# Log-sum-exp of 16,384 rows: 116 rows to a partition and 12 read last, instead of 112 and 16

## The chip, the cores and the metric

The kernel runs on one NeuronCore of one Trainium2 chip. The metric is the device time of one execution in microseconds (us). Before the change the median of three runs is 162.66 us (162.47 to 162.76). A profile adds one more execution, recorded by the hardware profiler.

Engines are named as in the profile: ACT (ScalarE: the exponentials and logarithms), DVE (VectorE: the sums), PE (TensorE: here only a tiny check), SP (SyncE, which issues the transfers; its queue is written SPq). Transfers run on 16 DMA engines of the core.

## The reference

The input has 32 x 512 = 16,384 rows of 1,024 float32 numbers (67.1 MB); the output is one float32 for each row.

```python
def reference(x):
    max_x = np.max(x, axis=-1, keepdims=True)
    return max_x.squeeze(-1) + np.log(np.sum(np.exp(x - max_x), axis=-1))
```

## The kernel before

**What it computes.** It takes exp without subtracting the maximum, sums each row and takes the logarithm. A check at the end looks whether every sum lies between 1e-15 and 1e15. If one doesn't, a slow path recomputes everything with the maximum; with the input used here it isn't taken.

**Rows and partitions.** There are 128 rows for each of 128 partitions (`NC = 128`; a row is 4 KB). `B` splits them. With B = 16, partition p holds rows 112p to 112p + 111 of the first 14,336 rows of the input (`x_rows`), so that its data begins 448 KB after that of partition p - 1. The last 2,048 rows of the input (`x_rest`) are spread 16 to a partition, and here partitions are 64 KB apart. `W = NC - B = 112` is the border, counted in rows of one partition; a load must lie on one side of it (the assertion in `source`). The output is cut in the same way, `out_rows` and `out_rest`.

**Loads.** The list `LOADS` gives eighteen transfers, all issued from SP into one ring of 48 rows for each partition. Each fetches the same number of rows for all 128 partitions, as one piece of consecutive bytes for each partition. I number them 1 to 18. Loads 1 to 4 have 16 rows (a 64 KB piece for a partition), load 5 has 13.5, load 6 12.5, load 7 9, load 8 7.5, load 9 5.5; that is 112 rows. Behind the border come 4.625 (load 10), 3.3125 (11), 2.4375 (12), 1.8125 (13), 1.3125, 0.9375, 0.5625, and the last row in two pieces of 0.625 and 0.375 (17 and 18). SP waits, before it issues a load, until the ring rows that it overwrites have been read (`load`).

**Work.** The string beside each size says what is done with the rows. "R8" is one exp on ACT over 8 rows and one reduction on DVE (lines 192 and 196). "T4" is one exp on ACT and four instructions on DVE, one for each row, each of which adds the halves of a row and accumulates (line 204). "A" is a single row where ACT accumulates the sum itself (line 181). "Y" and "Z" are the two pieces of the last row (line 170). The last exp of a load runs to the end of what has landed, so it may go over part of the row that the next load completes. ACT waits for a load's semaphore before its first exp.

**The end.** When row 119 of a partition (`LATE`) is summed, an early logarithm over the first W rows is put into ACT's order (line 219; it waits for the sums of the rows below the border), and the check of the first 119 sums into DVE's. SP then stores `out_rows` (line 227). After the last rows there are the logarithm of the other rows but one (line 230), that of the last row (line 232), the store of `out_rest` (line 236), and, beside these, the check of the last sums over DVE and PE. The program ends when the store has landed and the check has been read.

Of the kernel before, what the change touches and what calls it, by code (L numbers as in the profile page):

```python
# [8 lines left out]

LOW, HIGH = 1e-15, 1e15  # L10
RING = 48
B = 16
LATE = 119


# [1 line left out]
LOADS = [  # L17
# [4 lines left out]
]  # L22

# [24 lines left out]
def kernel(  # L48
# [21 lines left out]
    H = d // 2  # L70
    W = NC - B
    LAST = NC - 1
# [290 lines left out]
```

## Time and profile before

| what | us |
|---|---|
| median of three runs | 162.66 |
| profiled execution | 163.04 |
| its span, from the first to the last instruction | 161.7 |
| DVE busy | 117.7 |
| ACT busy | 116.9 |
| share of the span in which the 16 DMA engines moved the kernel's data | 97.2% |

The profiled execution took 1.3 us more than its span, and 0.38 us more than the median of the runs. Times in the views are counted from the start of the span. In the timeline a row is: start, duration, engine, line, operation, output and input with their shapes, count, and in brackets how long the engine was idle before and what it waited for. Where ACT was idle for a load, the start of its exp tells when that load landed, to some 0.02 us.

### The profile page before, as it was taken

To read this page: it belongs to the slowest core of one execution; us is meant where nothing else is said; L and a number is where in the kernel's file an instruction comes from. 1 tells how busy PE (TensorE), PEld (TensorE's weight loads), DVE (VectorE), ACT (ScalarE), POOL (GpSimd) and SP (SyncE) were. 2 spreads that over 40 slices of the span, in tenths; PEclk is the share of its full clock that TensorE was granted. 3 is DMA by queue.
4 is the path that set the end of the run, shared out by engine and by line. 5 is a ranking of instruction groups with operands and counts; after the bars stand their busy time and mean duration, and the time that the engine had idled before them with its cause. 6 is when DMAs were issued, how large, how long until landed. Compare 5 with 4: busy or idle time off the path is not lost.

```text
span 161.7 us, 249 instructions
## 1 busy us (share of the span) xinstructions
PE 2.1 (1%) x24; PEld 1.0 (1%) x24; DVE 117.7 (73%) x69; ACT 116.9 (72%) x55; POOL 0.2 (0%) x4
## 2 busy tenths in 40 slices
PE   0000000000000000000000000000000000000022
PEld 0000000000000000000000000000000000000011
DVE  0000000899929999399999999999399956999894
ACT  3000059980899609994299949973999999989986
POOL 0000000000000000000000000000000000000000
DMA  7997997998999899799699999998999999999990
GB/s 276 503 519 324 454 519 324 454 519 373 405 519 422 357 519 454 324 519 454 284 438 438 438 422 405 443 494 368 438 438 441 410 417 418 450 408 418 410 392 15
DMA packets 2881, 67.18 MB, mean 416 GB/s; under 512 B 576, under 2 KB 704, under 8 KB 1344
## 3 DMA queue, kind: packets, MB, share of 16 engines
q1 hardware_dynamic: 2880, 67.18, 97.2%
q14 instruction: 1, 0.01, 0.0%
HBM read 67.11 MB, written 0.07 MB: 415 GB/s over the span
## 4 chain that ended last, share of the span: by engine, by line
DMA 58%; ACT 19%; DVE 16%; another core or an unknown queue 3%; SPq 1%; issue 0%; PE 0%; DVEq 0%
DMA ring<-in_x_dram 58%; ACT ring L192 19%; DVE sumexp L196 15%; DVE ring L204 1%; SPq L126 0%; PE count L147 0%; PE count L248 0%; DVE clamped L242 0%; DVE fine L251 0%; SPq L44 0%; DVEq L44 0%
## 5 line engine op out<-in xcount | busy, mean ns | idle before, releaser
L192 ACT ACTIVATE ring<-ring 128x8192 f32<-128x8192 f32 (+18 forms) x27 | 103.6, 3891 | 41.8 <-DMA ring<-in_x_dram 41.8
L196 DVE TENSOR_REDUCE sumexp<-ring 128x8 f32<-128x8192 f32 (+6 forms) x17 | 102.9, 6107 | 39.2 <-ACT ring L192 39.2
L204 DVE SCALAR_TENSOR_TENSOR ring<-ring 128x512 f32<-128x512 f32 x22 | 14.1, 687 | 1.3 <-ACT ring L192 1.3
L181 ACT ACTIVATE ring<-ring 128x1024 f32<-128x1024 f32 x10 | 10.4, 1042 | 0.0
L114 ACT ACT_TABLE_LOAD x1 | 1.3, 1283 | 1.5 <-PEq L57 1.5
L143 PE MATMUL count<-far,bad 128*1 128x1 f32 x2 | 0.2, 164 | 153.8 <-DVE clamped L138 153.8
L181 ACT ACTIVATION_READ_ACCUMULATOR ring<-ring 128x1 f32 x10 | 1.9, 187 | 0.0
L204 DVE DVE_READ_ACCUMULATOR ring<-ring 128x1 f32 x22 | 1.8, 82 | 0.0
L147 PE MATMUL count<-sumexp,ones 128*1 128x1 f32 x20 | 1.8, 164 | 4.1 <-DVE ring L204 4.1
L170 ACT ACTIVATE last_exp<-ring 128x640 f32<-128x640 f32 (+1 forms) x2 | 1.2, 590 | 0.0
L115 DVE MEMSET ones<- 128x1 f32 x1 | 0.1, 59 | 1.5 <-PEq L57 1.5
L143 PEld LDWEIGHTS count<-far,bad 128*1 128x1 f32 x2 | 0.1, 80 | 153.8 <-DVE clamped L138 153.8
L147 PEld LDWEIGHTS count<-sumexp,ones 128*1 128x1 f32 x20 | 0.8, 81 | 5.1 <-DVE ring L204 4.9
L251 DVE TENSOR_SCALAR fine<-count 1x1 int32<-1x1 f32 x1 | 0.1, 145 | 0.5 <-PE count L147 0.5
L170 ACT ACTIVATION_READ_ACCUMULATOR last_exp<-ring 128x1 f32 x2 | 0.4, 186 | 0.0
L138 DVE SCALAR_TENSOR_TENSOR clamped<-clamped,sumexp 128x119 f32<-128x119 f32 x1 | 0.3, 282 | 0.0
L232 ACT ACTIVATE res<-sumexp 128x1 f32<-128x1 f32 x1 | 0.3, 294 | 0.0
L219 ACT ACTIVATE res<-sumexp 128x112 f32<-128x112 f32 x1 | 0.3, 279 | 0.0
L242 DVE SCALAR_TENSOR_TENSOR clamped<-sumexp 128x9 f32<-128x9 f32 x1 | 0.2, 169 | 0.1
L133 DVE TENSOR_SCALAR clamped<-sumexp 128x119 f32<-128x119 f32 x1 | 0.2, 223 | 0.0
L230 ACT ACTIVATE res<-sumexp 128x15 f32<-128x15 f32 x1 | 0.2, 198 | 0.0
L248 PE MATMUL count<-far,bad 128*1 128x1 f32 x2 | 0.2, 164 | 0.0
(8 smaller groups left out, 0.7 us busy)
## 6 DMA issues: line engine op xcount, KB each, us to landing
ring<-in_x_dram SPq DMA_DIRECT2D x1, 6912.0 KB, 31.8
ring<-in_x_dram SPq DMA_DIRECT2D x1, 6400.0 KB, 26.6
ring<-in_x_dram SPq DMA_DIRECT2D x1, 4608.0 KB, 25.2
ring<-in_x_dram SPq DMA_DIRECT2D x1, 3840.0 KB, 23.6
ring<-in_x_dram SPq DMA_DIRECT2D x1, 2816.0 KB, 26.0
ring<-in_x_dram SPq DMA_DIRECT2D x1, 2368.0 KB, 30.4
ring<-in_x_dram SPq DMA_DIRECT2D x1, 1696.0 KB, 23.1
ring<-in_x_dram SPq DMA_DIRECT2D x1, 1248.0 KB, 25.7
```

What stands on the lines that cost most here:

```text
L114: nc.scalar.preload_act_table_set("natural_log_exp_and_others")
L133: dve.did(nc.vector.tensor_scalar(out=clamped[:, 0:LATE], in0=sumexp[:, 0:LATE], scalar1=LOW, scalar2=HIGH, op0=ALU.max, op1=ALU.min,))
L138: dve.did(nc.vector.scalar_tensor_tensor(out=clamped[:, 0:LATE], in0=clamped[:, 0:LATE], scalar=0.0, in1=sumexp[:, 0:LATE], op0=ALU.bypass ...
L143: pe.did(nc.tensor.matmul(count, lhsT=bad[:, 0:1], rhs=far, start=True, stop=False))
L147: return pe.did(nc.tensor.matmul(count, lhsT=ones, rhs=sumexp[:, c : c + 1], **kw))
L170: at = act.did(nc.scalar.activation(out=last_exp[:, here - p : end - p], in_=ring[:, here:end], func=AF.Exp, accum_out=sumexp[:, LAST : NC ...
L181: at = act.did(nc.scalar.activation(out=v, in_=v, func=AF.Exp, accum_out=sumexp[:, c : c + 1]))
L192: at = act.did(nc.scalar.activation(out=v, in_=v, func=AF.Exp))
L196: who = (dve, dve.did(nc.vector.reduce_sum(out=sumexp[:, c : c + s], in_=rows, axis=AX.X)))
L204: who = (dve, dve.did(nc.vector.scalar_tensor_tensor(out=lo, in0=lo, scalar=1.0, in1=rows[:, r, H:d], op0=ALU.mult, op1=ALU.add, accum_out ...
L219: ln_early = act.did(nc.scalar.activation(out=res[:, 0:W], in_=sumexp[:, 0:W], func=AF.Ln))
L232: ln_last = act.did(nc.scalar.activation(out=res[:, LAST:NC], in_=sumexp[:, NC : NC + 1], func=AF.Ln, bias=sumexp[:, LAST:NC]))
```

## The change

B becomes 12, so that W becomes 116. Partitions of the first part are now 464 KB apart in the input, and those of the rest 48 KB. Load 10 has to end at the border and shrinks to 4 rows; load 11 becomes 3.5625 and load 12 2.8125. The rows up to the end of load 9 (112) and up to the end of load 12 (122.375) are as before, and so are all other sizes and the work on each row. Which rows of the input a load fetches does change, for all loads.

```diff
-B = 16
+B = 12
 LATE = 119
...
-    (4.625, "T4"), (3.3125, "T3"), (2.4375, "T3"), (1.8125, "T2"), (1.3125, "T1"), (0.9375, "T1"),
+    (4, "T4"), (3.5625, "T3"), (2.8125, "T3"), (1.8125, "T2"), (1.3125, "T1"), (0.9375, "T1"),
     (0.5625, "T1"), (0.625, "Y"), (0.375, "Z"),
```

By that the early logarithm covers 116 columns instead of 112, the late one 11 instead of 15. The first store writes 464 bytes for each partition instead of 448, the last store 48 instead of 64. In the instruction streams of the engines nothing else moves: PE and DVE have the same instructions in the same order, ACT and SP the same order with those sizes (and in the slow path, which isn't run, one transfer is cut at another row).

## The prediction

> **What bounds the kernel now.** I read the page's sums first, then ACT's timeline at the moments where it waits for data, then the transfers and the timeline of the last 20 us.
>
> ```profile
> span 161.7 us, 249 instructions
> PE 2.1 (1%) x24; PEld 1.0 (1%) x24; DVE 117.7 (73%) x69; ACT 116.9 (72%) x55; POOL 0.2 (0%) x4
> q1 hardware_dynamic: 2880, 67.18, 97.2%
> DMA 58%; ACT 19%; DVE 16%; another core or an unknown queue 3%; SPq 1%; issue 0%; PE 0%; DVEq 0%
> ```
>
> No engine is busy for three quarters of the span, while the DMA engines are at 97.2%. The chain that ended last names DMA for only 58%, because it walks back through the ring's free rows (DVE's reduction lets SP issue); that doesn't make DVE a bound, since a load is issued well before its data can start to flow. ACT's timeline shows the pace:
>
> ```profile
> 21.83 7.03 ACT L192 ACTIVATE ring<-ring 128x8192 f32<-128x8192 f32 x1 [19.09 <-DMA ring<-in_x_dram]
> 41.17 7.03 ACT L192 ACTIVATE ring<-ring 128x8192 f32<-128x8192 f32 x1 [5.21 <-DMA ring<-in_x_dram]
> 60.52 7.03 ACT L192 ACTIVATE ring<-ring 128x8192 f32<-128x8192 f32 x1 [5.31 <-DMA ring<-in_x_dram]
> 79.88 5.32 ACT L192 ACTIVATE ring<-ring 128x6144 f32<-128x6144 f32 x1 [5.41 <-DMA ring<-in_x_dram]
> 96.30 4.47 ACT L192 ACTIVATE ring<-ring 128x5120 f32<-128x5120 f32 x1 [2.38 <-DMA ring<-in_x_dram]
> 111.60 5.75 ACT L192 ACTIVATE ring<-ring 128x6656 f32<-128x6656 f32 x1 [3.39 <-DMA ring<-in_x_dram]
> 143.97 4.15 ACT L192 ACTIVATE ring<-ring 128x4736 f32<-128x4736 f32 x1 [0.43 <-DMA ring<-in_x_dram]
> ```
>
> Each start is a landing. Loads 2, 3 and 4 (16 rows) took 19.34, 19.35 and 19.36 us: 1.209 us for a row of each partition, or 8.389 MB / 19.35 us = 434 GB/s. Three equal steps speak of a ceiling without disturbance. Load 5 (13.5 rows) took 16.42 us, where 1.209 a row makes 16.32: 0.10 too many. Load 6 (12.5 rows) took 15.30 against 15.11: 0.19 too many. Loads 7 to 10 together (26.625 rows) took 32.37 against 32.19. So the stream runs from the first to the last microsecond, within about 1% of its best pace, and a change of its pace goes into the time one to one.
>
> The end of the span, in the same view:
>
> ```profile
> 148.18 3.03 ACT L192 ACTIVATE ring<-ring 128x3392 f32<-128x3392 f32 x1
> 151.12 0.28 ACT L219 ACTIVATE res<-sumexp 128x112 f32<-128x112 f32 x1
> 151.31 2.27 ACT L192 ACTIVATE ring<-ring 128x2496 f32<-128x2496 f32 x1
> 154.10 1.75 ACT L192 ACTIVATE ring<-ring 128x1856 f32<-128x1856 f32 x1 [0.53 <-DMA ring<-in_x_dram]
> 158.54 0.71 ACT L170 ACTIVATE last_exp<-ring 128x640 f32<-128x640 f32 x1
> 159.91 0.29 ACT L232 ACTIVATE res<-sumexp 128x1 f32<-128x1 f32 x1
> 160.23 0.34 SPq L236 DMA_DIRECT2D out_dram<-res  x1
> ```
>
> From 154.10 on ACT has no gap: load 13's landing, then 6.1 us of ACT work, then the last store. Load 13 is late by its own measure. By the transfers' view load 12 was issued at 125.47 and took 25.7 us (151.17), load 13 at 125.94 and 28.1 us (154.04 to 154.08). That is 2.9 us for 1.8125 rows, which at 1.209 make 2.19. The transfers between 152.1 and 152.5 us name the cause that I suspect, a foreign packet on one DMA engine:
>
> ```profile
> q1 hardware_dynamic: 29, 0.18, 115.0%
> q14 instruction: 1, 0.01, 4.8%
> ```
>
> 4.8% of 16 engines' 0.4 us is 0.31 us of one engine, for fetched instructions.
>
> **The change, part by part.**
>
> *Rows 0 to 111 with partitions 464 KB apart instead of 448 (loads 1 to 9).* The bytes, pieces and order are the same; only addresses move. No row of this trace has the new pitch, so I bound it by loads that step in similar ways. A DMA engine goes from the end of one partition's piece to the start of the next. In loads 1 to 4 that step is 448 - 64 = 384 KB, six times 64 KB exactly. In load 5 it is 394 KB, in load 6 398 KB, no multiples of 64 KB, and these are the two long loads that lost time: 0.29 us in 26 rows, 0.011 us a row. With the new pitch loads 1 to 4 step by 400 KB, so they lose that regularity. At 0.011 us a row, 64 rows cost +0.7 us. The rows don't all agree: load 7 steps by 412 KB, was issued at 97.25 and took 25.2 us (to 122.45), which is 10.85 us for 9 rows, no loss at all. The high end is load 6's 0.015 a row over 112 rows, +1.7. Further out lies load 11, 4.22 us for 3.3125 rows (issued 125.09, 23.1 us later landed), 0.065 a row; over 64 rows that would be +4.2. The low end is that all of what loads 5 to 10 lose goes: 0.10 + 0.19 + 0.18 = -0.47. I take +0.7, by loads 5 and 6, the nearest in piece size and the only ones long enough to be measured well.
>
> The Trainium skill's page "DMA: Bandwidth & Descriptors", section "Latency and other measured facts", speaks against this: there, copies slowed down when the row pitch was a large power of two (207 GB/s at 512 KiB, 103 at 4 MiB), and 4 KiB of padding on the 4 MiB pitch brought the full rate back. Neither 448 nor 464 KB is such a power, and 464 KB is divisible by 16 KB at most where 448 is by 64, so by that rule the new pitch is no worse, and the sum would be that of the rivals below, 0 or a gain. The three 19.35 us steps agree that 448 KB does no harm, and no run here shows 464.
>
> *Rows behind the border, partitions 48 KB apart instead of 64, and loads 10 to 12 of other sizes.* The bytes up to load 9 and up to load 12 are the same, so on the old pace load 10 lands 0.625 x 1.209 = 0.76 us earlier (143.2), load 11 0.375 x 1.209 = 0.45 earlier (147.7), and load 12 at 151.17 as before. ACT: load 10's exp is 128x4096 (3.60 us by the row of that shape) from 143.56, where ACT becomes free, to 147.15; then it waits for load 11. That exp is 128x3648: 3.03 + 256 x (4.15 - 3.03)/1344 = 3.24 us, from 147.7 to 150.95. The early logarithm, 116 columns for 112, at the old 0.28. It needs the four sums of load 10; DVE finishes the sums of load 9 at 147.9, then four at 0.61 each, 150.3: no wait. Load 12's exp is 128x2880: 2.27 + 384 x 0.00083 = 2.59 us from 151.19, and leaves ACT free for the next at about 153.70 (successive exps overlap by some 0.08), where before it was free at 153.50. Load 13 lands at 154.08, so this 0.20 is hidden by the wait of 0.53. If that cover goes, because load 13 lands on pace at 151.17 + 2.19 = 153.36, the 0.20 stands in the time in full. I take 0, and keep 0 to +0.2. DVE's three sums behind load 12 then begin at 153.8 instead of 153.67 and end at 155.7; the next ones wait for ACT until 155.89 already. SP's waits for ring rows move with the pieces: loads 11 to 13, issued at 125.09 to 125.94 behind DVE's reduction, begin to flow some 18 us later, and load 10 was issued 30.4 us before it landed. That cover is too large to vanish.
>
> The foreign packet stays, I suppose; instruction streams are nearly the same. If it falls on a DMA engine that is ahead of the others, load 13 lands earlier, and ACT, free at 153.70, gains at most 154.10 - 153.72 = 0.38. I take 0 and keep -0.4.
>
> *The end.* The late logarithm has 11 columns instead of 15, 0.20 us either way (a one-column one took 0.29, by another form). The last store has 48-byte pieces at addresses 48 bytes apart. The old one took 1.4 us from issue to landing; its packets, 144 with 4.6% of 16 engines' 2 us, about 10 ns each. Were each twice as long, nine on an engine would add 0.1; faster by more than a few hundredths it can't be, with less than 0.1 us of packets on an engine. I take 0, and keep 0 to +0.1. The first store, issued behind all loads, landed 7.8 us later at 159.2, before the last one is even issued: nothing.
>
> Sum: +0.7 + 0 + 0 + 0 = +0.7 us on the profiled 163.04, so 163.74. Since the profiled run lies 0.38 above the median, that is 163.36 for the median; I say 163.35.
>
> **The rivals.**
>
> *Pace unchanged.* The stream is at the same ceiling for 64 KB, 36 KB and 30 KB pieces, at five different offsets within a partition, and load 7's odd step costs nothing. Then only the tail is left: 0 to +0.3 us, 162.66 to 162.96. For it: the three equal steps; against it: load 6's 0.19.
>
> *Faster.* The old pitch, 448 KB, puts all partitions at multiples of 64 KB; if the losses of loads 5 to 10 come from engines that meet in the same place of DRAM, addresses spread over multiples of 16 KB take them away. It decides from a loss of under 0.14 us left of the 0.47, and gives up to 162.19 (162.66 - 0.47). This is also where the Trainium skill's rule on row pitch leads when it is taken further than its figures go. Against it: loads 2 to 4 have nothing to gain, and they are half of the stream. The foreign packet on another engine would give the same size, 162.3.
>
> *Much slower.* The new pitch disturbs all loads as load 11 was disturbed: 0.065 x 64 = +4.2, 166.9. Only one short load speaks for it.
>
> **How the numbers follow.** No change means within 0.2%, 0.33 us, about what a measurement of this kernel can tell. Stalls in the first loads, +0.35 to +1.7: 0.42, the forecast. Pace unchanged: 0.28. Faster by 0.33 or more: 0.22, gain of pitch and of packet together. Much slower: 0.08. So faster 0.22, same 0.28, slower 0.50. The range goes from 162.25, which leaves out the far part of the gain, to 164.5 (1.7 for the pitch and the tail's 0.1 or 0.2, on 162.66), which leaves out the much slower case and little else. The forecast case's own range is 163.0 to 164.4.
>
> **What would show it.** In the changed profile ACT's waits for loads 2, 3, 4 should be about 19.5 us apart instead of 19.35; equal steps of 19.35 mean that the pitch costs nothing and that the forecast is wrong. The step from 79.88 to 111.60 (31.72 us for loads 5 and 6) shows the opposite: 31.4 would be the gain. Load 12's exp should start at its landing with load 11's done 0.1 to 0.2 us earlier, and the wait before load 13's exp should shrink from 0.53 to about 0.4. The last store should take 1.4 us to land. What would make me wrong most is the address map of DRAM, of which this trace shows one pitch only.

## The result and the profile after

| | us, median (lowest to highest) |
|---|---|
| before | 162.70 (162.47 to 163.08) |
| after | 163.02 (162.71 to 163.30) |

The ratio is 1.0020, with a 95% interval of 1.0014 to 1.0026: slower by 0.33 us (0.23 to 0.42). The forecast was +0.7, the range 162.25 to 164.5. The sign and the range hold. The mechanism that I had forecast doesn't, as the profile of the changed kernel shows at once. Its execution took 162.97 us. First the page:

```profile
span 161.6 us, 249 instructions
PE 2.1 (1%) x24; PEld 1.0 (1%) x24; DVE 117.5 (73%) x69; ACT 116.7 (72%) x55; POOL 0.2 (0%) x4
q1 hardware_dynamic: 2880, 67.18, 97.2%
DMA 57%; DVE 19%; ACT 18%; another core or an unknown queue 3%; issue 0%; SPq 0%; PE 0%; DVEq 0%
```

The sums agree within 0.2 us, and the DMA engines' share is the same. Then ACT's timeline, where each start is the landing of a load (loads 1 to 6):

```profile
22.30 7.03 ACT L192 ACTIVATE ring<-ring 128x8192 f32<-128x8192 f32 x1 [19.56 <-DMA ring<-in_x_dram]
41.62 7.03 ACT L192 ACTIVATE ring<-ring 128x8192 f32<-128x8192 f32 x1 [5.18 <-DMA ring<-in_x_dram]
60.98 7.03 ACT L192 ACTIVATE ring<-ring 128x8192 f32<-128x8192 f32 x1 [5.32 <-DMA ring<-in_x_dram]
80.33 5.32 ACT L192 ACTIVATE ring<-ring 128x6144 f32<-128x6144 f32 x1 [5.40 <-DMA ring<-in_x_dram]
96.67 4.47 ACT L192 ACTIVATE ring<-ring 128x5120 f32<-128x5120 f32 x1 [2.30 <-DMA ring<-in_x_dram]
111.80 5.75 ACT L192 ACTIVATE ring<-ring 128x6656 f32<-128x6656 f32 x1 [3.22 <-DMA ring<-in_x_dram]
```

Loads 2, 3 and 4 step by 19.32, 19.36 and 19.35 us, where I had written that equal steps of 19.35 mean that the forecast is wrong. The large term, stalls in the first loads, isn't there. Instead load 1 lands 0.47 us later than before (22.30 against 21.83), and loads 5 and 6 together take 31.47 us against 31.72.

The end of ACT's timeline:

```profile
147.79 3.24 ACT L192 ACTIVATE ring<-ring 128x3648 f32<-128x3648 f32 x1 [0.56 <-DMA ring<-in_x_dram]
150.94 0.28 ACT L219 ACTIVATE res<-sumexp 128x116 f32<-128x116 f32 x1
151.25 4.24 ACT L192 ACTIVATE ring<-ring 128x2880 f32<-128x2880 f32 x2
159.43 0.29 ACT L232 ACTIVATE res<-sumexp 128x1 f32<-128x1 f32 x1
```

The last store in SP's timeline:

```profile
159.75 0.34 SPq L236 DMA_DIRECT2D out_dram<-res  x1
```

And the same store in the view of transfers, where the last two columns are its size and the us from issue to landing:

```profile
out_dram<-res SPq DMA_DIRECT2D x1, 6.0 KB, 1.9
```

The last logarithm starts at 159.43, which is 0.48 us *earlier* than in the first profile of before (159.91), and the span is nevertheless hardly shorter (161.6 against 161.7). The last store took 1.9 us where the old one took 1.4. The old one's row, from the first profile of before:

```profile
out_dram<-res SPq DMA_DIRECT2D x1, 8.0 KB, 1.4
```

So two theories stood at this point. **Store:** the 48-byte store lands later, and that is the whole loss. **Pitch:** the 0.4 to 0.5 us at load 1 go through to the end, and the 1.9 is chance. The first profile of before, with its late load 13, was under suspicion in either.

### The profile page after: what moved, and what is told of

It is laid out like the page before. It is cut to its first block, busy times and chain, and to the rows that moved or that the text cites. A ratio compares the mean times of both kernels' runs of the same rounds, so it can differ in the third digit from the quotient of the medians.

```text
span 161.6 us, 249 instructions
## 1 busy us (share of the span) xinstructions
PE 2.1 (1%) x24; PEld 1.0 (1%) x24; DVE 117.5 (73%) x69; ACT 116.7 (72%) x55; POOL 0.2 (0%) x4
## 4 chain that ended last, share of the span: by engine, by line
DMA 57%; DVE 19%; ACT 18%; another core or an unknown queue 3%; issue 0%; SPq 0%; PE 0%; DVEq 0%
DMA ring<-in_x_dram 57%; ACT ring L192 18%; DVE sumexp L196 15%; DVE ring L204 3%; SPq L126 0%; PE count L248 0%; DVE clamped L242 0%; PE count L147 0%; DVE fine L251 0%; SPq L44 0%; DVEq L44 0%
## 5 line engine op out<-in xcount | busy, mean ns | idle before, releaser
L192 ACT ACTIVATE ring<-ring 128x8192 f32<-128x8192 f32 (+17 forms) x27 | 103.3, 3889 | 41.6 <-DMA ring<-in_x_dram 41.5
## 6 DMA issues: line engine op xcount, KB each, us to landing
ring<-in_x_dram SPq DMA_DIRECT2D x1, 1440.0 KB, 25.6
```

The lines of the kernel that those rows point to most:

```text
L192: at = act.did(nc.scalar.activation(out=v, in_=v, func=AF.Exp))
```

## The experiments

Ratios are to the kernel before, run beside each on the same chip.

**r1: the kernel before once more.** No edit.

> The kernel before, unchanged, for a second profile of it. In the first one load 13 landed 2.9 us after load 12 (2.19 on pace) with a foreign packet beside it, load 1 landed at 21.83, and the last store took 1.4 us from issue to landing. Every theory: ratio 1.000 within 0.001. If the late load 13 of the first profile is a matter of where the foreign packet falls, it may be gone here, the span then 161.2 to 161.4; if it belongs to the program, load 13 again lands 2.8 to 2.9 us after load 12. The store theory needs 1.4 us again for the last store.

Ratio 0.9998 (0.9989 to 1.0007), span 161.4. Landings of loads 4 and 6, and the wait ahead of load 13's exp:

```profile
79.87 5.32 ACT L192 ACTIVATE ring<-ring 128x6144 f32<-128x6144 f32 x1 [5.41 <-DMA ring<-in_x_dram]
111.35 5.75 ACT L192 ACTIVATE ring<-ring 128x6656 f32<-128x6656 f32 x1 [3.23 <-DMA ring<-in_x_dram]
153.82 1.75 ACT L192 ACTIVATE ring<-ring 128x1856 f32<-128x1856 f32 x1 [0.64 <-DMA ring<-in_x_dram]
```

Loads 5 and 6 take 31.48 us. All other profiles with the 448 KB pitch have 31.46 to 31.48 too. The 0.29 us that I had read as the price of a step that is no multiple of 64 KB were an event of that one execution, and the "gain" of the changed kernel in these loads was its absence. Load 13 is late again (3.0 us after load 12: 125.22 + 25.6 and 125.69 + 28.1 in the transfers' rows). It isn't in every run: in r3, r6 and r10 below, whose loads are those of before, load 13 comes 2.26 to 2.29 us after load 12, and load 14 is the late one (2.14 to 2.25 us after load 13, where r1 has 1.66). In these three the foreign packet starts at 152.6 to 152.9 us, in the other profiles with this pitch at 150.8 to 152.3. So a late load near the end belongs to the program, and which one it is goes with when the packet comes. The last store took 1.4 us again.

**r2 and r3: the two halves of the change apart.** A second constant cuts the output independently of the input. r2 has the loads of after and the stores of before, r3 the reverse.

```diff
-B = 16
+B = 12          # r2; in r3 B stays 16
+BO = 16         # r2; in r3 12
...
+    WO = NC - BO
-    out_rows = out_flat[0 : P * W].rearrange("(p c) -> p c", p=P)
-    out_rest = out_flat[P * W : n].rearrange("(p c) -> p c", p=P)
+    out_rows = out_flat[0 : P * WO].rearrange("(p c) -> p c", p=P)
+    out_rest = out_flat[P * WO : n].rearrange("(p c) -> p c", p=P)
```

The logarithms and stores use `WO` in place of `W`, and r2 has the sizes of loads 10 to 12 of after.

> Loads of the changed kernel (464 KB and 48 KB pitch, new sizes), stores of the kernel before (448 and 64 bytes for a partition). The sums are right, but are stored at the places of the other cut. Store theory (the 48-byte store costs the 0.45 us that the last store took longer): last store 1.4 us, time as before or slightly less, ratio 0.998 to 1.000. Pitch theory (load 1 lands 0.45 us later because partitions 464 KB apart start worse, and that goes through): ratio 1.002, load 1 at 22.3 us, the store as in the changed kernel or not is of no matter.

> Loads of the kernel before, stores of the changed one (464 and 48 bytes for a partition; early logarithm over 116 columns). The output is permuted. Store theory: last store 1.8 to 1.9 us from issue to landing, ratio 1.002 to 1.003. Pitch theory: last store of 48 bytes is a chance event, ratio 1.000, load 1 at 21.8 us.

r2: 0.9995 (0.9985 to 1.0004). Load 1 landed at 22.2 us, so the late start is there, and the time is that of before. r3: 1.0019 (1.0010 to 1.0028), with load 1 at 21.9. The stores alone cost what the whole change costs, and the loads alone nothing measurable. The transfers' row of the last store in r2, and then in r3:

```profile
out_dram<-res SPq DMA_DIRECT2D x1, 8.0 KB, 1.4
```

```profile
out_dram<-res SPq DMA_DIRECT2D x1, 6.0 KB, 1.6
```

They were issued at 159.73 and 159.77 us; the spans are 161.2 and 161.4. The store theory holds, though r3's 1.6 us is less than the 1.8 to 1.9 that it had asked for, and the pitch theory falls. r3 also has the changed kernel's first store. That one isn't in the way: in the changed kernel's two profiles and in r3 it had landed by 158.74 to 158.83 us, 1.0 us before the last store was issued.

**r4: the sizes of loads 10 to 12 alone.**

```diff
-    (4.625, "T4"), (3.3125, "T3"), (2.4375, "T3"),
+    (4, "T4"), (3.5625, "T3"), (2.8125, "T3"),
```

> The kernel before with loads 10 to 12 of 4, 3.5625 and 2.8125 rows; pitch and stores as before (the load that ends at 116 rows lies behind the border of 112 as the old one did). Store theory and pitch theory: ratio 1.000. Tail theory (ACT is free for load 13 0.20 us later, and the cover of that is absent in most runs): ratio 1.001 to 1.0015, and ACT without a wait ahead of load 13's exp.

Ratio 0.9998 (0.9989 to 1.0007). The wait ahead of load 13's exp shrinks from r1's 0.64 to 0.28 and so still covers the longer exp of load 12:

```profile
153.70 1.75 ACT L192 ACTIVATE ring<-ring 128x1856 f32<-128x1856 f32 x1 [0.28 <-DMA ring<-in_x_dram]
```

The tail theory gives no measurable cost; the 0 that I took for this term stands.

**r5, r6: what makes the store slow.** In r5 the pieces are 48 bytes, but 64 apart; in r6 64 bytes, but shifted by 16.

```diff
# r5
-    nc.sync.dma_start(out=out_rest, in_=res[:, W:NC])
+    nc.sync.dma_start(out=out_rest[:, 4:16], in_=res[:, W + 4 : NC])
# r6
-    out_rest = out_flat[P * W : n].rearrange("(p c) -> p c", p=P)
+    out_rest = out_flat[P * W - 4 : n - 4].rearrange("(p c) -> p c", p=P)
```

> The kernel before, but its last store writes only the last 12 of its 16 columns: pieces of 48 bytes that begin 64 bytes apart, 16 bytes behind a multiple of 64; 512 results are left out. Theory of shared lines (a 48-byte pitch makes pieces of different partitions fall into the same 64 bytes, and their writes get in each other's way): 1.4 us from issue to landing, ratio 1.000. Theory of partial lines (a piece that doesn't fill its 64 bytes is slow by itself): 1.6 to 1.9 us, ratio 1.002.

> The kernel before, but its last store goes to addresses 16 bytes lower, so that each 64-byte piece covers parts of two 64-byte lines and shares both with its neighbours; the first store leaves out 4 columns to make room (432 of 448 bytes for a partition), and some results stand in the wrong place or are missing. Both theories of the store (shared lines, partial lines): 1.6 us or more from issue to landing, ratio 1.001 to 1.003. If only the size of a piece counts: 1.4 us, ratio 1.000.

r5: 1.0000 (0.9991 to 1.0009). r6: 1.0004 (0.9995 to 1.0013). The transfers' row of the store in r5, and then in r6:

```profile
out_dram<-res SPq DMA_DIRECT2D x1, 6.0 KB, 1.4
```

```profile
out_dram<-res SPq DMA_DIRECT2D x1, 8.0 KB, 1.5
```

A piece of 48 bytes isn't slow by itself; the theory of partial lines falls with r5. Pieces that share lines at 64 bytes' length took 0.1 us more in r6, less than both theories had asked for, in one profile and with a time that can't be told from that of before.

**r9, r10: how wide the sharing has to be.** r9 puts the 48-byte pieces 96 bytes apart, r10 shifts the 64-byte pieces by 128 bytes.

```diff
# r9
-    out_rest = out_flat[P * W : n].rearrange("(p c) -> p c", p=P)
+    out_rest = out_flat[P * (W - 8) : n].rearrange("(p c) -> p c", p=P)
...
+    nc.sync.dma_start(out=out_rest[:, 0:12], in_=res[:, W + 4 : NC])
# r10
+    out_rest = out_flat[P * W - 32 : n - 32].rearrange("(p c) -> p c", p=P)
```

> The kernel before, but its last store writes 12 columns as 48-byte pieces that begin 96 bytes apart; the first store writes 104 columns, to make room, and results stand in other places or are missing. Here no two pieces touch the same 64 bytes, but the four neighbouring partitions that one DMA engine should be writing cover 384 bytes, so that blocks of 256 bytes are written by two engines. Theory of shared 64-byte lines: 1.4 us from issue to landing. Theory of blocks of 256 bytes (or 512) that two DMA engines write at once: 1.5 to 1.9 us.

> The kernel before, but its last store goes to addresses 128 bytes lower: 64-byte pieces that fill whole 64-byte lines as before, while the 256 bytes of four neighbouring partitions now straddle two blocks of 256. The first store leaves out 32 columns; results stand in other places. Theory of shared 64-byte lines: 1.4 us from issue to landing, as before. Theory of blocks of 256 bytes that two DMA engines write at once: 1.5 to 1.9 us.

r9: 1.0003 (0.9993 to 1.0013), r10: 1.0001 (0.9991 to 1.0010). Both stores took 1.4 us, so blocks of 256 bytes written from two sides don't matter. Taken together, with places counted from the start of the output:

| last store | run | two pieces in the same 64 bytes | issue to landing, us |
|---|---|---|---|
| 64 bytes, 64 apart | before, r1, r2, r4, r7, r11, r12 | no | 1.4 in each |
| 48 bytes, 48 apart | after, r3, r8 | yes | 1.9, 1.6, 1.6 |
| 48 bytes, 64 apart | r5 | no | 1.4 |
| 48 bytes, 96 apart | r9 | no | 1.4 |
| 64 bytes, 64 apart, shifted 128 | r10 | no | 1.4 |
| 64 bytes, 64 apart, shifted 16 | r6 | yes | 1.5 |

In the trace each store's semaphore is raised sixteen times, once for each DMA engine. The first raise comes 1.25 to 1.27 us after the issue in all of them. The last comes 1.40 to 1.43 us after it without shared lines, 1.52 us in r6, 1.61 us in r3 and r8 and 1.86 us after the change. So some of the engines get their confirmation late (later than 1.43 us: 8 of the sixteen after the change, 7 in r3 and in r8, 2 in r6), and the rest aren't touched. Sharing a 64-byte line is a condition that fits every row of the table. Lines of 32 bytes would fit as well, since the pieces that share 64 bytes here share 32 too, and no run separates the two; lines of 128 bytes wouldn't, since the 64-byte pieces of before share those and took 1.4 us. The place that the store reads from isn't the cause: r5 and r9 read the same 48 bytes of each partition as the changed kernel. Why it costs 0.1 us at 64 bytes and 0.2 to 0.45 at 48 stays open.

**r7, r11, r12: the pitch of the first 112 rows alone.** Loads read the first 112 of every 116, 128 or 113 rows; all else is as before.

```diff
-    x_rows = x_flat[0 : P * W].rearrange("(p c) d -> p (c d)", p=P)
+    x_rows = x_flat[0 : P * PITCH].rearrange("(p c) d -> p (c d)", p=P)   # 116, 128, 113
```

> The kernel before with partitions 464 KB apart for the first 112 rows (four rows between them are skipped, and 512 rows are read from elsewhere, so that those results are not the reference's); sizes, the last 16 rows and the stores as before. Pitch theory: load 1 lands at 22.2 us instead of 21.8, and loads up to 12 keep that 0.4. If it went through to the end: ratio 1.0025. If the foreign packet near load 13 is hidden behind the DMA engine that is late from the start: load 13 lands at 153.6, 2.4 us after load 12 instead of 2.9, and the ratio is 1.000.

> The kernel before with partitions 512 KB apart for the first 112 rows (512 rows of each 2048 are not those of the reference). Theory that the pitch matters only for the first pieces, where all DMA engines start together: load 1 lands somewhere between 21.8 and 22.4 us, the steps of 19.35 stay, ratio 0.998 to 1.002. Theory of the forecast (a pitch with worse meetings of the engines in DRAM slows all pieces): steps of loads 2 to 4 of 19.5 us and more, ratio over 1.004. By the Trainium skill, page DMA: Bandwidth & Descriptors, section Latency and other measured facts, a pitch of 512 KiB was slightly slower than a padded one (207 against 214 GB/s); were it so here, the ratio would be about 1.03, as an estimate from that page.

> The kernel before with partitions 452 KB apart for the first 112 rows, a multiple of 4 KB alone (one row in 113 is skipped). Theory of the first pieces: load 1 lands at another time than 21.8 us, by up to 0.5 us, the steps of 19.35 stay, ratio 0.998 to 1.002. Theory of the forecast: a step between pieces that is no multiple of 64 KB costs 0.1 us and more for each of loads 2 to 4, ratio over 1.003.

r7 (464 KB): 0.9989 (0.9980 to 0.9998). r11 (512 KB): 1.0018 (1.0005 to 1.0030). r12 (452 KB): 0.9999 (0.9989 to 1.0008). Landings of loads 1, 2, 4 and 6 with 464 KB:

```profile
22.40 7.03 ACT L193 ACTIVATE ring<-ring 128x8192 f32<-128x8192 f32 x1 [19.66 <-DMA ring<-in_x_dram]
41.72 7.03 ACT L193 ACTIVATE ring<-ring 128x8192 f32<-128x8192 f32 x1 [5.19 <-DMA ring<-in_x_dram]
80.42 5.32 ACT L193 ACTIVATE ring<-ring 128x6144 f32<-128x6144 f32 x1 [5.41 <-DMA ring<-in_x_dram]
111.89 5.75 ACT L193 ACTIVATE ring<-ring 128x6656 f32<-128x6656 f32 x1 [3.22 <-DMA ring<-in_x_dram]
```

From load 1 to load 4 these are 58.02 us, against 58.05 before, and 31.47 from there to load 6. The pitch costs some 0.5 us once, at the start, and nothing per byte. By the landings in the trace, load 1 is complete at 22.20 to 22.38 us in all four profiles with 464 KB, at 21.79 to 21.95 in the eight with 448 KB, at 21.86 with 452 KB and at 22.32 with 512 KB. The first of the sixteen DMA engines is done with load 1 at 21.2 to 21.4 us in every profile, so it is not the whole load that comes later but the slowest engines. At 512 KB the steps to load 4 sum to 58.27, so 0.2 us more on the way, in one profile; loads 5 and 6 then take 31.47 us as elsewhere, so whether that is a loss per byte stays open.

And the 0.5 us of the start are gone at the end. In r7 load 12 lands at 151.32 us and load 13 at 153.58, 2.26 us later, close to the pace of 2.19. r7's expectation had named that time, with the packet hidden behind the late engine at load 13. That isn't how it came: here the foreign packet starts at 152.42 us, and the load that comes with a second late engine is load 14. The raises of the loads' semaphores, sixteen for each load, show what happens. In r1 those of load 12 lie within 0.44 us; at load 13 fifteen lie within 0.40 us and one comes 1.17 us behind the first, so one DMA engine has lost 0.7 us or more, and it is still as late at load 18. In r7 one engine is late from the start: at load 12 it comes 1.05 us behind the first, and the next at 0.59. At load 14 there are two, at 1.03 and 1.12. A load is complete with its slowest engine, so the two delays lie side by side and don't add: load 14 is complete at 155.31 us in r7 and at 155.46 in r1. That it is the foreign packet that holds up the second engine is argued from its time and not shown, since the profile doesn't name the engine of a packet.

**r8: the changed kernel once more.**

> The changed kernel, unchanged, for a second profile and next to the others on the same chip. Store theory: last store 1.6 to 1.9 us, ratio 1.002, all of it in the store: the last logarithm starts no later than in the kernel before. Pitch theory: load 1 at 22.2 to 22.3 us again. The gain in loads 5 and 6 of its first profile (31.47 us for both against 31.72) should not be a gain of the pitch, since the second profile of the kernel before has 31.48.

Ratio 1.0012 (1.0002 to 1.0023), load 1 at 22.2 us, and the last store:

```profile
out_dram<-res SPq DMA_DIRECT2D x1, 6.0 KB, 1.6
```

With the last logarithm at 159.51 us against 159.59 in r1, everything up to the store is on time, and the store is late. Its times go from 162.63 to 163.39 us, while r7, with the same pitch and the old store, stays within 162.51 to 162.65. That fits a store whose landing varies from execution to execution, as the 1.6 and 1.9 us do.

## Why the prediction was right in sign and wrong in its reasons

- *Rows 0 to 111 at 464 KB, +0.7 us:* wrong. Measured, the loads of after cost -0.08 us (r2; -0.24 to +0.07), the pitch alone -0.18 (r7; -0.33 to -0.03). The step that failed is the choice of the nearest row: loads 5 and 6 of one profile. The three equal steps of 19.35 us, the row with the larger sample, stood beside it, and so did load 7, which contradicted the reasoning about steps.
- *The low end, a gain of 0.47:* the same 0.29 of it was chance. The other 0.18, in loads 7 to 10, is there in r1 and in r7 alike (32.37 and 32.38 us), so the pitch doesn't touch it, and there was nothing of that kind to gain.
- *The Trainium skill's rule* (page "DMA: Bandwidth & Descriptors", section "Latency and other measured facts"), by which 464 KB was no worse than 448, was right for the pace where I set it aside: the steps at 464 KB are those at 448. Its 207 against 214 GB/s at 512 KiB would make some 3%, as an estimate; r11 measured 0.18% there. The direction agrees, the size doesn't; this kernel loads into on-chip memory, where that table has copies within DRAM.
- *The tail:* right in its sum. Load 11's exp took 3.24 us as worked out and waited as forecast. In the sizes alone (r4) the wait ahead of load 13 covers the longer exp of load 12. In the changed kernel load 13 lands a little earlier, at 153.63, and its exp starts at 153.76 without the wait of about 0.4 us that I had named: there about 0.1 of my 0.20 lies bare, inside what r2 couldn't tell from nothing.
- *The foreign packet:* it stays, as supposed. The time went the way of "-0.4", by less: load 14 is complete at 155.26 us after the change, and at 155.46 (r1) and 155.77 before. That the late start lies beside the delay of another engine and so costs nothing at the end, I hadn't foreseen.
- *The last store, 0 to +0.1:* the term that decided, and mis-sized. I had said that it would land in 1.4 us; measured +0.2 in two profiles and +0.45 in one. I had bounded it by the packets' own time, 10 ns each, and those are as short as before. The delay lies between the packets and the confirmations, in a part of the store's 1.4 us that no packet row shows.
- *The rivals:* "pace unchanged" describes the loads behind the first. Its upper end of 162.96 is near the measured 163.02, but by the tail, which costs nothing, and not by the store. So the forecast of "slower" came true through a term that I had priced at zero, and that the sign and the range hold is luck.

No version that beats both kernels was found. r7's 0.9989 comes from a kernel that skips rows; with every row read, a 464 KB pitch leaves 12 rows to a partition and so the 48-byte last store.

## What to carry to other kernels

A store that ends a kernel counts from issue to its last confirmation; lay it out so that no two pieces lie in the same 64 bytes, even if another layout moves fewer bytes (here 48-byte pieces 48 bytes apart took 0.2 to 0.45 us longer than 64-byte pieces). When a change moves a split point, follow it to every transfer that uses it: the output's cut decided here, not the input's, which the change was described by. And a deviation of 1% in one profile is to be seen twice before a mechanism is built on it; where a longer and steadier row says zero, that one is the better price.

## What was not expected of the hardware

- Stores of pieces that share 64-byte lines (32 bytes would fit as well) are confirmed late on some DMA engines: 1.52 to 1.86 us from the issue instead of 1.40 to 1.43, with packets equally short (10 ns).
- The pitch between partitions acts on the first pieces: load 1 was complete 0.2 to 0.6 us later at 464 and 512 KB than at 448 or 452 KB (one profile each at 452 and 512), while pieces after the first run at one pace (19.35 us for 16 rows) at 448, 452 and 464 KB.
- A late DMA engine at the start of a stream doesn't catch up, and the lateness was still there 129 us later, at load 12, but it didn't add to a delay of another engine (load 14 at 155.31 us in r7, at 155.46 in r1).
